# Hybrid trunk layer: one division per pair of attention heads, mixer A's scores in bank pairs, keys stacked by transfers

## The chip, the cores and the metric

The kernel runs on one core of one Trainium2 chip. A core has TensorE (PE, matrix multiplies into PSUM; its weight loads are shown as PEld), VectorE (DVE), ScalarE (ACT), GpSimd (POOL) and SyncE (SP), which here only issues transfers. The metric is the device time of one execution in microseconds (us). Before the change it is 999.15 us, the median of three runs (996.32 to 1001.0).

## What is computed

One layer of a transformer-like trunk for 640 tokens (128 context tokens, 512 latent tokens on a grid of 8 by 64), width 1024. After a modulated RMSNorm one projection gives queries, keys and values of two attention mixers (A: 8 query heads on 2 key heads; B: 8 heads, a 2-D neighbourhood with a learned bias) and two gates. Latent queries also read 128 cached context keys. The outputs of both mixers are merged under the gates, and an MLP follows.

```
def one(qblk):                                     # mixer A, 128 queries at a time
    s = einsum('bqgrd,bkgd->bgrqk', qblk, k) * scale
    p = softmax(s, axis=-1)
    return einsum('bgrqk,bkgd->bqgrd', p, v)
...
p = softmax(concatenate([s_loc, s_ctx], axis=-1))  # mixer B, per grid row
o = einsum('bhqn,bnhd->bqhd', p[..., :n_loc], vr)
return o + einsum('bhqk,bkhd->bqhd', p[..., n_loc:], ctx_v)
...
m = sigmoid(ga) * (a_o @ w_br_a) + sigmoid(gb) * (b_o @ w_br_b)
x = x + g1 * (m @ w_out)
x = x + g2 * _mlp(_rmsnorm(x, n2) * (1 + sc2) + sh2, w1, w2)
```

## The kernel before

Activations lie with features on the 128 partitions and the 640 tokens along the free axis, in two halves of 320 (`HT`, `HALVES`). Matrix products are made from float32r parts: each operand is split into a high and a low part (`wh`, `wl`, `h..h`, `h..l`), and `gemm_k` (L335) makes three matmuls of 320 columns for each of eight blocks of 128 features, so 24 matmuls make one half of a weight tile and 48 a tile. A weight tile is loaded by SP (`wst`), its high part written by ACT (L301), its low part by POOL or DVE (L302). Up to three tiles are held.

In order of the program: a first stage projects the tiles of mixer A's keys, first query pair and values (`FIRST`) while the modulation is computed; the attention stage follows (L504 to L957); then merge, output projection and MLP (from L960).

The attention stage is a list of units: for each pair j of heads `HeadA(2j)`, `HeadA(2j+1)` and the context queries `CtxPair("a", j)`, then the same for B. `attention` (L922) walks in steps. In one step it writes down a T of the unit before, an S of the unit at hand, the value product (`pv`) left by the last step, and then filler.

- S (L630, L686): scores of 128 latent queries against 640 keys (A) or 384 to 512 (B) on PE, the row maximum on DVE, `exp` with the row sum on ACT, and `normalise` (L617), in which DVE takes the reciprocal of the sum and multiplies the whole row block `pa` or `pb` by it. A's scores lie in two single banks, so maximum and `exp` come in two pieces that small DVE operations put together (L643, L646).
- T (L651, L705): PE transposes four blocks of 128x128 into the bank `pt`, ACT and DVE split them into `ph` and `pl`, and `pv` multiplies them by the values into `po`. After a head's last `pv`, `combine` (L611) adds the two halves of `po` into `AO` or `BO`.
- Filler (`fill_tile`, L789) is the projection of tiles that come later: 19 tiles, of which `GATES` are stored to memory for the merge. `STEP` says how much filler a step gets.

PSUM has eight banks in one pool `pp`: two of `g` (projections), three of `s` (scores), two of `t` (transposes), one of `o` (`po`). Keys are needed twice over, on partitions 0 to 63 and 64 to 127, for each of two heads: `k_both` (L569) writes both copies for A by ACT and DVE, in pieces of 64 partitions; `k_part` and `k_dup` write one for B and copy it by a transfer on POOL's queue.

The code is no fixed order in this stage: a scheduler of the framework orders the instructions of every engine by the written order and by when it reckons their inputs ready. Each engine then takes its list in order, and an instruction that waits holds up all that stand behind it on its engine.

## Time and profile before

| what | us |
|---|---|
| median of three runs | 999.15 |
| the profiled execution | 996.88 |
| its span, first to last instruction | 994.9 |
| first stage, until the filler begins | 55.8 |
| start of attention, until the first score | 19.9 |
| units of mixer A | 141.9 |
| units of mixer B, and on to the merge's first product of attention outputs | 145.4 |
| merge, output projection, MLP | 632 |

The stages were cut where PE changes its work: the first filler matmul starts at 55.8 us, the first score (L640) at 75.7, the first score of B (L693) at 217.6, the first matmul that reads a split attention output (`osh`) at 362.9. A profile is read here from the engine with the most work: for each stage, how long PE was idle, what ended each wait, and at what clock it ran. "Granted clock" (PEclk) is 1.00 at full speed.

### The profile page before, as it was taken

How to read it: one execution, taken by the hardware profiler on the slowest of the kernel's cores; microseconds unless marked ns; L12 is line 12 of the kernel's file. 1: busy time of each engine (PE TensorE's matmuls, PEld its weight loads, DVE VectorE, ACT ScalarE, POOL GpSimd, SP SyncE). 2: the span in 40 equal slices, each digit the busy share in tenths (PEclk: the TensorE clock that was granted, in tenths of full speed). 3: DMA queues.
4: the chain of work that ended last, by engine and by line, in shares of the span. 5: the costliest groups of instructions: out<-in, count | busy, mean ns of one | idle time of the engine just before them, and what ended most of it. 6: DMA issues, size and time to landing. Idle time of an engine off the chain costs nothing.

```text
span 994.9 us, 16602 instructions
## 1 busy us (share of the span) xinstructions
PE 950.5 (96%) x6343; PEld 907.5 (91%) x6343; DVE 703.6 (71%) x1577; ACT 517.0 (52%) x1117; POOL 172.0 (17%) x153
## 2 busy tenths in 40 slices
PE   8979899998899999999999999999999999999996
PEld 7767778887788999999999999999999999999996
DVE  4578777788866788788677786778833884368644
ACT  5475667666655654644433564247611663156542
POOL 0351233111222010200041200012200220012100
PEclk9998999999999999999999999999999999999998
DMA  9952110312542455654742253312321233121313
GB/s 345 213 185 58 31 44 25 77 41 80 135 105 76 133 173 172 222 164 155 240 127 86 65 158 110 89 48 85 105 74 35 86 106 88 62 73 34 110 39 107
DMA packets 34768, 108.49 MB, mean 109 GB/s; under 512 B 4320, under 2 KB 8032, under 8 KB 34688
## 3 DMA queue, kind: packets, MB, share of 16 engines
q1 hardware_dynamic: 27072, 82.63, 26.7%
q0 software_dynamic: 6464, 23.47, 8.0%
q8 instruction: 50, 0.82, 0.4%
q10 hardware_dynamic: 1152, 1.31, 0.4%
q14 instruction: 30, 0.25, 0.1%
HBM read 99.14 MB, written 4.60 MB: 104 GB/s over the span
## 4 chain that ended last, share of the span: by engine, by line
PE 68%; DVE 14%; ACT 8%; DMA 5%; issue 4%; POOL 1%; SPq 0%; POOLq 0%; ACTq 0%; DVEq 0%
PE pg L339 7%; PE pg L340 7%; PE pss L341 7%; PE pg L341 7%; PE pss L340 7%; PE pss L339 7%; PE pt L340 4%; PE pt L341 4%; PE pt L339 4%; DMA ms<-wmodA 3%; DVE sr L260 3%; ACT wb L280 2%; PE pt L654 1%; ACT wh L301 1%; DMA wst<-w 1%
## 5 line engine op out<-in xcount | busy, mean ns | idle before, releaser
L301 ACT ACTIVATE wh<-wst 128x1024 fp32r<-128x1024 f32 x84 | 88.8, 1057 | 113.7 <-PE pg L340 41.3
L302 DVE TENSOR_TENSOR wl<-wst,wh 128x1024 fp32r<-128x1024 f32 x53 | 64.8, 1222 | 63.2 <-ACT wh L301 63.1
L302 POOL TENSOR_TENSOR wl<-wst,wh 128x1024 fp32r<-128x1024 f32 x31 | 74.6, 2407 | 158.0 <-ACT wh L301 158.0
L993 DVE SCALAR_TENSOR_TENSOR mt<-wmt,cb 128x512 f32<-128x512 f32 x128 | 81.4, 684 | 0.0
L281 POOL TENSOR_TENSOR wb<-wst,wb 128x512 fp32r<-128x512 f32 x24 | 31.8, 1323 | 260.6 <-ACT wb L280 236.2
L341 PE MATMUL pss<-hidh,wl 128*128 128x320 f32 x216 | 67.0, 310 | 3.4 <-POOL wl L302 3.4
L339 PE MATMUL pss<-hidh,wh 128*128 128x320 f32 x216 | 66.7, 309 | 0.0
L340 PE MATMUL pss<-hidl,wh 128*128 128x320 f32 x216 | 66.7, 309 | 0.0
L608 DVE TENSOR_TENSOR pl<-pt,ph 128x512 fp32r<-128x512 f32 (+2 forms) x80 | 50.2, 632 | 19.5 <-ACT ph L607 18.3
L607 ACT ACTIVATE ph<-pt 128x512 fp32r<-128x512 f32 (+2 forms) x80 | 44.3, 555 | 31.7 <-PE pt L654 15.9
L280 ACT ACTIVATE wb<-sr 128x512 fp32r<-128x512 f32 x48 | 29.8, 626 | 51.5 <-DVE sr L260 37.6
L1162 DVE TENSOR_TENSOR hidl<-rl,hidh 128x320 fp32r<-128x320 f32 x64 | 37.4, 585 | 20.7 <-ACT hidh L1155 20.2
L989 POOL DMA_DIRECT2D wmt<-wmodB x32 | 17.2, 538 | 170.4 <-DVE mt L993 103.3
L281 DVE TENSOR_TENSOR wb<-sr,wb 128x512 fp32r<-128x512 f32 x48 | 36.0, 754 | 14.3 <-ACT wb L280 14.1
L339 PE MATMUL pg<-hidh,wh 128*128 128x320 f32 x144 | 44.5, 309 | 0.0
L340 PE MATMUL pg<-hidl,wh 128*128 128x320 f32 x144 | 44.5, 309 | 0.0
L341 PE MATMUL pg<-hidh,wl 128*128 128x320 f32 x144 | 44.5, 309 | 0.0
L341 PEld LDWEIGHTS pss<-hidh,wl 128*128 128x128 f32 x216 | 40.5, 188 | 4.2 <-POOL wl L302 4.2
L339 PE MATMUL pt<-hidh,wh 128*128 128x320 f32 x136 | 42.0, 309 | 0.0
L340 PE MATMUL pt<-hidl,wh 128*128 128x320 f32 x136 | 42.0, 309 | 0.0
L341 PE MATMUL pt<-hidh,wl 128*128 128x320 f32 x136 | 42.0, 309 | 0.0
L645 ACT ACTIVATE pa<-pss,nm 128x320 f32<-128x320 f32 x64 | 33.2, 524 | 16.3 <-DVE nm L643 16.1
(958 smaller groups left out, 3459.2 us busy)
## 6 DMA issues: line engine op xcount, KB each, us to landing
wst<-w SPq DMA_DIRECT2D x64, 512.0 KB, 3.6
wmt<-wmodB POOLq DMA_DIRECT2D x32, 512.0 KB, 4.1
wst<-w_in SPq DMA_DIRECT2D x31, 512.0 KB, 3.9
ms<-wmodA SPq DMA_DIRECT2D x16, 512.0 KB, 7.5
x<-xT SPq DMA_DIRECT2D x16, 320.0 KB, 6.3
bt<-bias SPq DMA_DIRECT2D x16, 320.0 KB, 3.0
wst<-w_br SPq DMA_DIRECT2D x8, 512.0 KB, 4.2
wst<-w_out SPq DMA_DIRECT2D x8, 512.0 KB, 3.5
```

Source lines behind the costliest of these rows:

```text
L280: ACT.activation(t[:, lo4], src, AF.Copy)
L281: later.append(lambda: (nc.gpsimd if name in BLKP else DVE).tensor_sub(t[:, hi4], src, r32(t[:, lo4])))
L301: ACT.activation(hi, st, AF.Copy)
L302: (nc.gpsimd if key in WPOOLSET else DVE).tensor_sub(lo, st, r32(hi))
L339: PE.matmul(ps, wh[:, k], xh[:, sl], start=first, stop=False)
L340: PE.matmul(ps, wh[:, k], xl[:, sl], start=False, stop=False)
L341: PE.matmul(ps, wl[:, k], xh[:, sl], start=False, stop=last)
L607: ACT.activation(ph[:, :n], pt[:, :n], AF.Copy)
L608: DVE.tensor_sub(pl[:, :n], pt[:, :n], r32(ph[:, :n]))
L645: ACT.activation(p[:, HALVES[j]], ps[j][:, :HT], AF.Exp, bias=nm, accum_out=s2[:, j:j + 1])
L993: DVE.scalar_tensor_tensor(t, st[:, q * 512:(q + 1) * 512], 1.0, r32(cb[2 * q + i][:, :512]), op0=OP.mult, op1=OP.mult, accum_out=parts[:, ...
L1162: DVE.tensor_sub(dst[1][:, sl], r[:, :HT], r32(dst[0][:, sl]))
```

## The change

- **Normalisation.** `normalise` is gone. `exp` writes its row sum into one column of an 8-column tile for the pair (`row_sum`). Once both heads have their sums, `pair_sums` takes one reciprocal and ACT lays it along the free axis as a 128x512 tile `rc`; `pair_norm` transposes `rc` by four PE transposes into a `pt` bank and DVE multiplies the pair's output by it. `rc` comes from the ring of five tiles (`r_`) that `ph`, `pl`, `ct` and `pc` use.
- **Bank pairs.** During mixer A PSUM is divided otherwise: two pairs of banks for scores, two `t`, one `o`, and one `g` instead of two. Maximum and `exp` of a block are one instruction each. With mixer B the old division returns.
- **Keys.** One 128-partition split (`k_split`) makes high and low parts, and six transfers (`k_stack`) lay the copies, on SP's queue for A and on POOL's for B. The cached keys are loaded into the same tile `kr`.
- **Order.** More filler is written ahead of the first score, the gates 21, 29 and 22 move into A's filler list and 30 to the head of B's, `spend` stops at the end of a half during A, squares of the queries are taken ahead of their product, and T is written after the filler. POOL's low parts of these tiles come in two halves. One subtraction for the first query pair moves from POOL to DVE (`Q0P`).

```diff
-AFILL = (1, 10, 2, 6, 3, 14, 21)
-BFILL = (11, 7, 15, 12, 8, 16, 13, 9, 17, 29, 22, 30)
+AFILL = (21, 29, 1, 10, 2, 6, 3, 14, 22)
+BFILL = (30, 11, 7, 15, 12, 8, 16, 13, 9, 17)
-STEP = 2050
-EARLY = 4000
+STEP = {"pa": 2100, "pp": 2500}
+UNIT = 440
-Q0P = 2
+Q0P = 0
...
+    BANKS = {"pp": {"g": 2, "s": 3, "t": 2, "o": 1}, "pa": {"S": 2, "t": 2, "o": 1, "g": 1}}
...
+    def ps_2():
+        return psum["p"].tile([P, 2, 512], F32, tag="S", bufs=2, name="pss")
...
+                    for ks in (slice(0, 4), slice(4, KT)) if key[0] == "in" else (slice(0, KT),):
+                        nc.gpsimd.tensor_sub(lo[:, ks], st[:, ks], r32(hi[:, ks]))
...
+    def k_split(src, n):
+
+        t = kt_tile("kh"), kt_tile("kl")
+        ACT.activation(t[0][:, :n], src[:, :n], AF.Copy)
+        DVE.tensor_sub(t[1][:, :n], src[:, :n], r32(t[0][:, :n]))
+        return t
+
+    def k_stack(t, own, n, q):
+
+        o = kt_tile("kh"), kt_tile("kl")
+        for e in (1 - own, own):
+            for i in range(2):
+                for f in range(2):
+                    if e != own or f != own:
+                        q[i].dma_start(r32((t if e == own else o)[i][half(f), :n]), r32(t[i][half(e), :n]))
+        return (o, t) if own else (t, o)
...
-    def normalise(p, sm):
-        rc = small("rc", 1)
-        DVE.reciprocal(rc, sm)
-        DVE.tensor_scalar(p, p, rc, None, op0=OP.mult)
...
+    def pair_sums(mixer, j):
+        RC[mixer, j] = r_("rc")
+        sm = SUMS[mixer, j]
+        DVE.reciprocal(sm, sm)
+        ACT.activation(RC[mixer, j].rearrange("p (q e d) -> p q e d", q=4, e=2),
+                       sm.rearrange("p (e q) -> p q e", e=2).unsqueeze(3).broadcast_to([P, 4, 2, 64]), AF.Copy)
+
+    def pair_norm(mixer, j):
+
+        rc, o = RC[mixer, j], (AO if mixer == "a" else BO)[j]
+        rows = ps_t()
+        for qt in range(4):
+            PE.transpose(rows[:, qt * P:(qt + 1) * P], rc[:, qt * P:(qt + 1) * P], ident)
+        DVE.tensor_mul(o[:, P:NT], o[:, P:NT], rows)
...
-                DVE.tensor_reduce(n2[:, j:j + 1], ps[j][:, :HT], axis=AX.X, op=OP.max, negate=True)
-            DVE.tensor_tensor(nm, n2[:, 0:1], n2[:, 1:2], op=OP.min)
-            for j in range(2):
-                ACT.activation(p[:, HALVES[j]], ps[j][:, :HT], AF.Exp, bias=nm, accum_out=s2[:, j:j + 1])
-            DVE.tensor_add(sm, s2[:, 0:1], s2[:, 1:2])
-            normalise(p, sm)
+            DVE.tensor_reduce(nm, ps, axis=AX.XY, op=OP.max, negate=True)
+            ACT.activation(p.rearrange("p (a b) -> p a b", a=2), ps, AF.Exp, bias=nm, accum_out=row_sum("a", self.hd, qt))
...
-            ACT.activation(p[:, :w], ps[:, :w], AF.Exp, bias=nm, accum_out=sm)
-            normalise(p[:, :w], sm)
+            ACT.activation(p[:, :w], ps[:, :w], AF.Exp, bias=nm, accum_out=row_sum("b", self.hd, qt))
...
+    ksq = [qk_squares(acc0[0][h], r_) for h in range(2)]
+    F.spend(3 * UNIT)
...
+    AK = k_stack(k_split(kraw, NT + P), 1, NT + P, (DQ[1],) * 2)
...
+    F.spend(6 * UNIT)
     AV, vp = v_stack(vraw, cv[:, 0:P], ps_t)
     for f in vp:
+        F.spend(4 * UNIT)
         f()
-    k_both(AK[1], 1, slice(NT, NT + P), ck[:, 0:P])
-    k_both(AK[1], 1, slice(0, NT), kraw)
-    F.spend(EARLY)
+    F.spend(13 * UNIT)
+    F.half_end()
+    open_banks("pa", "pa")
```

Three places show what this does to the engines' lists. The first is PE at the first scores of mixer A. `pg<-h..,w..` is filler, `pss<-...qs` a score. Before:

```order
L341 MATMUL pg<-h7h,wl 128x320
L640 MATMUL pss<-akh,qs 128x320
L641 MATMUL pss<-akl,qs 128x320
L640 MATMUL pss<-akh,qs 128x320
L641 MATMUL pss<-akl,qs 128x320
L640 MATMUL pss<-akh,qs 128x320
L641 MATMUL pss<-akl,qs 128x320
L535 MATMUL pg<-qsq,pk 128x320
L339 MATMUL pg<-h0h,wh 128x320
```

And now:

```order
L362 MATMUL pg<-h7h,wl 128x320
L687 MATMUL pss<-kh,qs 128x320
L688 MATMUL pss<-kl,qs 128x320
L687 MATMUL pss<-kh,qs 128x320
L688 MATMUL pss<-kl,qs 128x320
L360 MATMUL pg<-h0h,wh 128x320
L361 MATMUL pg<-h0l,wh 128x320
```

Ahead of the first row of scores stood 72 filler matmuls (three halves); now 120 stand there (five halves), and filler comes already after the first block's four score matmuls.

The second place is DVE in mixer A, at the end of the first pair of heads. `n` and `nm` are maxima, `sm` and `s` sums, `pl` the low part of transposed probabilities, `ao` the output. Before:

```order
L642 TENSOR_REDUCE n_1308<-pss 128x1
L608 TENSOR_TENSOR pl<-pt,ph 128x512 x2
L643 TENSOR_TENSOR nm<-n_1308 128x1
L642 TENSOR_REDUCE n_1357<-pss 128x1
L608 TENSOR_TENSOR pl<-pt,ph 128x512
L646 TENSOR_TENSOR sm<-s_1309 128x1
L619 RECIPROCAL rc<-sm 128x1
L620 TENSOR_SCALAR pa<-pa,rc 128x640
L608 TENSOR_TENSOR pl<-pt,ph 128x512
```

And now:

```order
L636 TENSOR_TENSOR pl<-pt,ph 128x512 x4
L689 TENSOR_REDUCE nm<-pss 128x1
L636 TENSOR_TENSOR pl<-pt,ph 128x256
L689 TENSOR_REDUCE nm<-pss 128x1
L643 TENSOR_TENSOR ao_906<-po,ct 64x512
L689 TENSOR_REDUCE nm<-pss 128x1
L643 TENSOR_TENSOR ao_906<-po,ct 64x128
L667 TENSOR_TENSOR ao_906<-ao_906,pt 128x512
```

The five operations that stood between a block's scores and its transposes, beside the maximum, are gone, and one product with the pair's reciprocals (L667) stands behind the pair's outputs.

The third place is PE at the end of the attention stage: the last value products of the context queries (`po<-pl,vst 128x256`) and the gate projections of the merge behind them. Before:

```order
L770 MATMUL po<-pl,vst 128x256
L340 MATMUL pss<-h7l,wh 128x320
L341 MATMUL pss<-h7h,wl 128x320
L339 MATMUL pt<-h0h,wh 128x320
L340 MATMUL pt<-h0l,wh 128x320
L341 MATMUL pt<-h0h,wl 128x320
L769 MATMUL po<-ph,vst 128x256
L770 MATMUL po<-pl,vst 128x256
```

And now:

```order
L666 MATMUL pt<-pk,rc 128x128 x4
L360 MATMUL pss<-h6h,wh 128x320
L361 MATMUL pss<-h6l,wh 128x320
L362 MATMUL pss<-h6h,wl 128x320
L360 MATMUL pss<-h7h,wh 128x320
L361 MATMUL pss<-h7l,wh 128x320
L362 MATMUL pss<-h7h,wl 128x320
L360 MATMUL pt<-h0h,wh 128x320
L819 MATMUL po<-ph,vst 128x256
```

Between the last value product and the first matmul that reads a split attention output stood 69 gate matmuls; now 42 stand there, since more of the gates' work has moved up among the last pair of heads, which have no filler tile left: all 912 filler matmuls stand ahead of the last head's last score, where before 24 were left.

More of the change, by code (lines that the diff above doesn't have):

```diff
@@ L510, in trunk_layer @@
     nc.sync.dma_start(sin, tabs[1])
-    ck, cv = (kp.tile([P, NT], F32, name=x) for x in ("ck", "cv"))
-    nc.sync.dma_start(ck, cacheK)
+    cv = kp.tile([P, NT], F32, name="cv")
     nc.sync.dma_start(cv, cacheV)
@@ L582, in v_cols, with v_stack @@
         return vv[:, :, 0:64], vv[:, :, 64:P]
-    def v_stack(raw, cvp, bank=ps_g):
+    def v_stack(raw, cvp, bank=ps_x):
         v = kp.tile([P, 6 * 256], F32R, tag="V", bufs=2, name="vst")
@@ L853, in __init__ @@
             self.todo = list(AFILL + BFILL)
-            self.allowed = len(AFILL)
+            self.allowed = len([n for n in AFILL if n not in GATES])
             self.cur = None
@@ L884, in spend, with half_end @@
                 self.debt -= c
+        def half_end(self):
+            while self.cur is not None and self.step():
+                pass
         def until(self, what):
@@ L924, in attention @@
         for cur_u in units + [None]:
+            if isinstance(cur_u, HeadB) and "S" in psum["n"]:
+                pend()
+                pend = None
+                F.half_end()
+                while after:
+                    after.pop(0)()
+                open_banks("pp", "pb")
             if cur_u is not None:
@@ L938, in attention @@
                 t, new = 0, None
-                if prev is not None and i < prev.nT:
-                    c, new = prev.T(i)
-                    t += c
+                todo, after[:] = list(after), []
                 if cur_u is not None and i < cur_u.nS:
                     t += cur_u.S(i)
+                tail = prev is not None and i < prev.nT
+                F.spend(max(0, STEP[psum["kind"]] - t - (520 if tail else 0) - (470 if pend else 0) - 500 * len(todo)))
+                if tail:
+                    _, new = prev.T(i)
                 if pend is not None:
-                    t += pend()
+                    pend()
+                for f in todo:
+                    f()
                 pend = new
-                F.spend(max(0, STEP - t))
             prev = cur_u
@@ L950, in attention @@
             pend()
+        while after:
+            after.pop(0)()
     todo = []
```

155 lines of the change are left out of this document (91 added, 64 removed).

## The prediction

> **What bounds the kernel now.** I read the page first, then the busy times of each engine cut at the stages, then who ended PE's waits in the attention stage, then the rows around its longest wait.
>
> ```profile
> span 994.9 us, 16602 instructions
> PE 950.5 (96%) x6343; PEld 907.5 (91%) x6343; DVE 703.6 (71%) x1577; ACT 517.0 (52%) x1117; POOL 172.0 (17%) x153
> ...
> 55.80:75.70 19.90, 13.80 (x87) 12.41 (x86) 15.62 (x25) 14.91 (x35) 9.57 (x8) 0.96 0.60 215
> 75.70:80.70 5.00, 5.00 (x17) 4.61 (x18) 3.13 (x9) 1.87 (x7) 0.00 (x0) 0.50 0.00 0
> 104.80:109.40 4.60, 3.33 (x15) 2.72 (x15) 2.85 (x9) 3.10 (x9) 2.99 (x2) 0.63 0.23 50
> 75.70:217.60 141.90, 129.40 (x776) 112.82 (x777) 114.73 (x301) 94.17 (x255) 34.57 (x24) 0.97 0.17 45
> 217.60:363.00 145.40, 137.48 (x891) 125.94 (x891) 108.26 (x293) 92.35 (x226) 27.39 (x27) 1.00 0.38 106
> 363.00:995.00 632.00, 618.64 (x4193) 615.17 (x4191) 436.69 (x895) 288.37 (x551) 85.41 (x75) 1.00 0.34 108
> ```
>
> The second group's columns: the stretch in us, its length, the busy time of PE, PEld, DVE, ACT and POOL (x instructions), the granted clock, the share of the DMA engines, GB/s. PE bounds the kernel: 96% busy over the span, and after 363 us it is idle for 632.00 - 618.64 = 13.4 us in 632. The change touches nothing there. What it can win lies in three stages: PE is idle for 6.1 us of the start, 141.90 - 129.40 = 12.5 us of mixer A, 145.40 - 137.48 = 7.9 us of mixer B. Twice the granted clock falls: 0.50 for the 5.0 us after the first score, which costs 2.5 us of work at full speed, and 0.63 for 4.6 us at 104.8, which costs 1.7. Together 30.7 us: no version of the attention stage with the same PE work can win more.
>
> ```profile
> PE pss L640 <- DVE qs L561: 6.1, 1, 6.1
> PE pt L654 <- DVE pa L620: 4.8, 9, 1.1
> PE pss L640 <- ACT pa L645: 3.0, 4, 1.4
> PE po L662 <- DVE pl L608: 1.9, 3, 1.0
> PE pt L654 <- DVE pl L608: 1.3, 1, 1.3
> ...
> PE po L769 <- DVE bo L615: 2.6, 2, 1.4
> PE po L662 <- DVE pl L608: 1.6, 1, 1.6
> PE pt L711 <- DVE nm L699: 1.6, 3, 0.9
> PE po L723 <- DVE pl L608: 1.1, 2, 0.9
> ```
>
> Each row is PE's waiter, who ended the wait, the sum in us, how often, the longest. The first five are A with the wait for its first score, the last four B. Nearly all name DVE, which is busy for 114.73 of A's 141.90 us (81%). The row for L620 is the multiplication by the reciprocal itself: the transposes of a block wait for it.
>
> **The start.** Before, the first score stands behind 72 filler matmuls and waits 6.1 us for a query part. DVE and POOL meanwhile:
>
> ```profile
> 67.64 0.82 DVE L574 TENSOR_TENSOR akl<-raw,akh 64x640 fp32r<-64x640 f32 x1
> ...
> 70.01 2.32 DVE L567 TENSOR_TENSOR akl<-ck,akh 64x128 fp32r<-64x128 f32 x1
> ...
> 74.82 0.82 DVE L561 TENSOR_TENSOR qs<-raw,qs 64x640 fp32r<-64x640 f32 x1
> ...
> 69.80 2.38 POOL L302 TENSOR_TENSOR wl<-wst,wh 128x1024 fp32r<-128x1024 f32 x1 [2.86 <-ACT wh L301]
> ...
> 98.31 0.31 PE L339 MATMUL pg<-h2h,wh 128*128 128x320 f32 x1
> ...
> 99.78 0.31 PE L340 MATMUL pg<-h5l,wh 128*128 128x320 f32 x1
> ...
> DMA to landing us min/median/max: 2.7/5.8/7.5
> ```
>
> The last two PE rows are the first and last of eleven filler matmuls in a row: (99.78 - 98.31) / 10 = 0.147 us each. Now 120 of them precede the first score, 48 more than before: 48 x 0.147 = 7.1 us of work, which now lies where PE waited 6.1. Is the new chain ready by then? Before, the first key half was split by 68.46 us; DVE then wrote the other key half's copies ahead of the query parts, which ended at 75.64. Those copies (0.82 us at 67.64, 2.32 at 70.01, two more before 74.82) are gone, 4 to 5 us of DVE, so the query parts end near 71 us. The four transfers for the first head's keys follow the split at some 67 us; copies of this kind from POOL's queue took 2.7 to 7.5 us to land (last row, L578), so they land between 71 and 76, and PE arrives at about 55.8 + 17.6 (filler) + 1.5 (norm products and transposes) + 0.8 (the clock at 0.96) = 75.7. I take no wait: **-6.1, and -2.5** for the clock behind it. If the transfers are as slow as the slowest row and queue, 2 us of wait come back; the ends are -9 and -4.
>
> A 64x128 subtraction took 2.32 us there, beside 0.27 elsewhere, while POOL worked from 69.80 to 72.18. The Trainium skill (GPSIMD Engine Reference, Specifications) says that POOL shares its SBUF interfaces with VectorE, in contention for operations with two SBUF inputs. The row agrees; by it the new key split and the query subtraction that comes to DVE could be held once by a half conversion, some 1.2 us by the row for a whole one, which is inside the range above.
>
> **Mixer A.** The durations (busy us in all, mean ns of one):
>
> ```profile
> L620 DVE TENSOR_SCALAR pa<-pa,rc 128x640 f32<-128x640 f32 x32 | 18.7, 584 | 0.3
> L619 DVE RECIPROCAL rc<-sm 128x1 f32<-128x1 f32 x64 | 10.1, 158 | 9.8 <-ACT pb L700 9.1
> L646 DVE TENSOR_TENSOR sm<-s 128x1 f32<-128x1 f32 x32 | 10.1, 314 | 3.2 <-ACT pa L645 3.1
> L643 DVE TENSOR_TENSOR nm<-n 128x1 f32<-128x1 f32 x32 | 7.0, 219 | 0.2
> L642 DVE TENSOR_REDUCE n<-pss 128x1 f32<-128x320 f32 x64 | 30.8, 484 | 11.0 <-PE pss L641 10.4
> L615 DVE TENSOR_TENSOR ao<-po,ct 64x512 f32<-64x512 f32 x8 | 5.4, 681 | 1.8 <-ACT ct L614 1.7
> L620 DVE TENSOR_SCALAR pb<-pb,rc 128x512 f32<-128x512 f32 x16 | 9.9, 618 | 0.1
> L620 DVE TENSOR_SCALAR pb<-pb,rc 128x384 f32<-128x384 f32 x16 | 8.5, 533 | 0.2
> ```
>
> DVE loses 18.7 of products, 32 x 0.158 = 5.1 of reciprocals, 10.1 and 7.0 of small additions. Sixty-four maxima of 320 columns become 32 of 640, which the trace does not show: one costs between 0.484 and 0.968 us, and I take 0.80, so 5.2 saved. It gains four products like the L615 row, 2.7. That is 43 us off 115, and A's DVE share falls to about 55%. So the 4.8 us of L620 go; the 3.0 us in which a score waits for an `exp` to free its bank are halved, as two blocks fit in the banks where one and a half did; the 3.2 us for `pl`, a product late in DVE's list, are halved too: 4.8 + 1.5 + 1.6 = 7.9 of the 12.5. The stall before 104.8 was one of these, so its clock goes as well: **-7.9 and -1.7** (ends -4.8 and -14.2).
>
> A clock rule is to be weighed here. The row first: the clock fell to 0.63 behind a wait of 1.4 us (the longest of L640 on ACT). The Trainium skill (TensorE: Matmul & The Clock Gate, Part 1: The HAM clock gate) has the clock fall after an idle window of about 3.4 us. By that only the start's 6.1 us would cost clock and the sum would be 1.7 us smaller; I go by the row.
>
> **Mixer B.** DVE loses 9.9 + 8.5 of products and 5.1 of reciprocals and gains 2.7. The waits for `pl` (1.6 + 1.1) are halved, the 1.6 us behind the bias loses the products that stood in its list, say 1.0, and the 2.6 us for `combine` stay, as `po` still has one bank: **-2.3** (ends 0 and -5.3).
>
> **What it adds.**
>
> ```profile
> 94.69 0.60 PE L654 MATMUL pt<-pk,pa 128*128 128x128 f32 x4
> 95.04 0.48 PE L661 MATMUL po<-ph,vst 128*128 128x512 f32 x1
> ...
> L814 ACT ACTIVATE raw<-pg 128x320 f32<-128x320 f32 x30 | 12.9, 433 | 4.3 <-PE pg L341 4.2
> L607 ACT ACTIVATE ph<-pt 128x512 fp32r<-128x512 f32 x56 | 33.3, 597 | 21.3 <-PE pt L654 15.9 <-PE pt L711 4.8 <-PE po L661 0.3
> ...
> 353.29 0.28 DVE L615 TENSOR_TENSOR bo<-po,ct 64x128 f32<-64x128 f32 x1 [0.90 <-ACT ct L614]
> ...
> 359.50 0.82 DVE L350 TENSOR_TENSOR osl<-ao,osh 128x640 fp32r<-128x640 f32 x1
> ...
> 352.67 0.28 PE L770 MATMUL po<-pl,vst 128*128 128x256 f32 x1
> ...
> 362.90 0.31 PE L339 MATMUL pss<-osh,wh 128*128 128x320 f32 x1
> ```
>
> Four transposes take 95.04 - 94.69 = 0.35 us, so the 32 new ones are **+2.8** of PE (none of it hidden, PE being the bound). Their ACT copy, 8 x 0.6, lies in ACT's idle third.
>
> One `g` bank: 15 halves of filler start in A, and each must wait until ACT has copied the half before it out (0.433, plus what stands ahead of it on ACT, such as one `ph` of 0.597). PE's new list has score, transpose or value work between any two of these halves, 0.7 to 2.6 us of it by the prices above, 1.6 on average. So most copies are covered; I take 0.2 us a half, **+3.0** (ends 0 and +13).
>
> The ring of five: `rc` holds one tile while `ph`, `pl` (twice) and `pc` fill the rest, so the next `pl` waits for a `pv`. This touches about four steps of each of eight pairs, most with filler beside it: **+1.0** (0 to 3). The last pair of B has no filler tile: **+1.5** (0 to 4).
>
> The end: the first merge product reads eight splits that DVE makes one after the other behind the last `combine`; the seventh ended at 359.50 + 0.82 = 360.3, 7.6 us after the last value product began (352.67), and PE came to it at 362.9. Now 42 instead of 69 gate matmuls lie between, 6.2 us instead of 10.2. The product needs the seventh split only at its tenth matmul, 1.3 us on, so cover is 6.2 + 1.3 + 0.1 = 7.6: just enough, **0** (to +1.3).
>
> **Sum:** -8.6 - 9.6 - 2.3 + 2.8 + 3.0 + 1.0 + 1.5 = -12.2. The profiled execution took 996.88 us, which gives 984.7; it lies 2.3 below the median of the runs, 999.15, which would give 987. I say **986**.
>
> **Rivals.** *The single bank takes it back (slower).* The place is A's filler: each half waits for its copy-out. The price is 15 times the copy's wait beyond what PE finds to do; if ACT comes to the copy 0.8 us later than PE needs it, this costs 12 us and the rest of the gain is gone; at 1.2 us, with the short cover of 0.7 us between two of the halves and clock losses behind each, 18 to 20: 1004. For it: ACT is 66% busy in A (94.17 of 141.90) and takes its list in order. Against it: PE's list leaves 1.6 us on average, and one combined `exp` replaces two.
>
> *DVE was not the cause.* If PE's waits only move from L620 to `exp` and `ph`, both on ACT, then A keeps its 12.5 us and B its 7.9, the start gains 8.6 and the additions cost 8.3: 997 by the profile's own time, 999 by the median, no change.
>
> *Everything opens.* If nearly all of the 20.4 us of idle time in A and B go and the copies are covered, 996.9 - 30.7 + 2.8 + 3 = 972.
>
> *The transfers are late.* As the key copies at their slowest, with the weight loads on SP's queue in front: the start gives 4 instead of 8.6 and the clock falls again, 991. This is inside my forecast's range.
>
> **How the numbers follow.** The forecast (978 to 993, the late transfers among it) has 0.60, everything opens 0.17, no change 0.15, slower 0.08. The range leaves out the slower case and half of no change: 972 to 999. A measurement of this kernel tells about 0.5% from no change, that is 994.2 to 1004.1. Faster by more: 0.60 + 0.17 = 0.77; within it 0.15 and an eighth of the slower case, 0.16; slower 0.07.
>
> **What would show it.** Right: the first score starts at 75 to 77 us with no wait of over 2 us before it and a clock near 1.00 behind it; PE's idle time in A is 4 to 8 us with L697 no longer waiting for DVE's products; DVE's share of A is near 55%; the first `osh` matmul starts 10 to 14 us earlier than 362.9; after it the two runs are alike. Wrong: waits of filler (L360, first block) on ACT's `raw` copies of several us in sum (the bank), a wait of PE on key transfers at the start, or a long idle stretch ahead of the first `osh`.

## The result, and the profile after

| | median us | lowest to highest | runs |
|---|---|---|---|
| before | 998.72 | 996.32 to 1001.0 | 4 |
| after | 975.64 | 974.41 to 977.37 | 4 |

The ratio is 0.977, with a 95% interval of 0.9743 to 0.9798: the change takes away 23.1 us. The forecast was 986, so the direction and the range (972 to 999) held, and the gain was nearly twice the 12.2 us of the sum. The profiled execution took 975.83 us, close to the median.

The first lines are those of the changed kernel's page, the second fence has its busy times by stage (stretch, length, PE, PEld, DVE, ACT, POOL, granted clock, DMA share, GB/s). The stages are cut as before: first filler, first score of A, first score of B, first matmul on a split attention output, end.

```profile
span 973.7 us, 16415 instructions
PE 944.0 (97%) x6375; PEld 909.6 (93%) x6375; DVE 650.7 (67%) x1335; ACT 503.1 (52%) x1030; POOL 184.5 (19%) x188
```

```profile
56.95:77.26 20.31, 20.31 (x135) 19.66 (x134) 12.35 (x20) 12.25 (x27) 13.34 (x13) 1.00 0.86 272
77.26:82.26 5.00, 5.00 (x37) 5.00 (x36) 1.65 (x2) 2.68 (x6) 0.28 (x1) 1.00 0.56 186
77.26:210.42 133.16, 124.65 (x791) 112.70 (x790) 85.27 (x139) 88.81 (x194) 36.30 (x33) 0.99 0.18 53
210.42:340.08 129.66, 128.58 (x860) 121.29 (x859) 83.08 (x210) 83.18 (x198) 34.57 (x48) 1.00 0.47 129
340.08:973.70 633.62, 619.77 (x4194) 615.19 (x4192) 441.60 (x902) 291.87 (x560) 85.20 (x75) 1.00 0.34 107
```

Length less PE's busy time is its idle time. At the start it went from 6.1 us to nothing (20.31 of 20.31), and the clock behind the first score is 1.00 where it was 0.50. In mixer A it went from 12.5 to 133.16 - 124.65 = 8.5 us, in mixer B from 7.9 to 129.66 - 128.58 = 1.1. The last stage is 633.62 us, 632.00 before.

What ended PE's waits (waiter, releaser, sum in us, times, longest), first in A, behind the "..." in B:

```profile
PE po L704 <- DVE ao L643: 2.0, 1, 2.0
PE pg L360 <- DVE qs L580: 1.9, 1, 1.9
PE pg L360 <- ACT kr L874: 1.2, 1, 1.2
PE pss L687 <- POOL qs L586: 1.0, 1, 1.0
PE pt L697 <- DVE pl L636: 0.6, 2, 0.4
PE pss L687 <- ACT pa L690: 0.5, 1, 0.5
PE po L704 <- ACT ph L635: 0.4, 1, 0.4
PE po L705 <- DVE pl L636: 0.2, 1, 0.2
PE pg L360 <- ACT raw L876: 0.2, 1, 0.2
...
PE po L769 <- DVE nm L746: 0.6, 1, 0.6
PE po L705 <- DVE pl L636: 0.2, 1, 0.2
PE pg L360 <- DVE vst L628: 0.2, 1, 0.2
```

The 4.8 us for the product are gone, and of the 3.0 us for the exponential 0.5 are left. The waits of the first filler matmul of a half (L360) have grown, to 1.9 + 1.2 + 0.2 = 3.3 us in A; before they were 1.3 (L339). New is the wait for `combine` in A, 2.0 us.

**Idle time is not all that PE loses.** The prediction's rows show that records of 0.31 us each start 0.147 us apart: they overlap, so a matmul can start late and no gap is seen. A second count avoids that. Each matmul is given the shortest pitch seen from its start to the next start: 0.147 us for 320 columns, other widths in proportion, 0.35 / 4 = 0.088 for a transposition. The sum of the pitches is the work, and the stretch less the work is what PE lost.

| stage, us | start | A | B | from first filler to first `osh` |
|---|---|---|---|---|
| length before | 19.9 | 141.9 | 145.4 | 307.2 |
| work before | 12.1 | 109.9 | 126.6 | 248.6 |
| lost before (of it idle) | 7.8 (6.1) | 32.0 (12.5) | 18.8 (7.9) | 58.6 (26.5) |
| length after | 20.3 | 133.2 | 129.7 | 283.1 |
| work after | 19.2 | 111.0 | 121.2 | 251.4 |
| lost after (of it idle) | 1.2 (0) | 22.1 (8.5) | 8.5 (1.1) | 31.8 (9.6) |

So the span fell by 21.2 us: 6.6 less lost at the start, 9.9 in A, 10.3 in B, 2.8 more work, 1.2 more until the first filler and 1.6 more in the last stage (58.6 - 31.8 - 2.8 - 1.2 - 1.6 = 21.2). Those last two are not from the change's steps as far as the runs tell: over all kernels below the first filler began at 55.0 to 58.4 us with the same work ahead of it. What the clock costs is part of what is lost: where the granted clock falls in the middle of these profiles, it falls to 0.50 for 3.41 us or a multiple of it, and 3.41 us at 0.50 cost 1.7 us of work.

### The profile page after: what moved, and what is told of

The parts are those of the page before. It is cut to its first block, busy times and chain, and to the rows that moved or that the text cites. A ratio compares the mean times of both kernels' runs of the same rounds, so it can differ in the third digit from the quotient of the medians.

```text
span 973.7 us, 16415 instructions
## 1 busy us (share of the span) xinstructions
PE 944.0 (97%) x6375; PEld 909.6 (93%) x6375; DVE 650.7 (67%) x1335; ACT 503.1 (52%) x1030; POOL 184.5 (19%) x188
## 4 chain that ended last, share of the span: by engine, by line
PE 72%; DVE 10%; ACT 7%; DMA 5%; issue 3%; POOL 1%; SPq 0%; POOLq 0%; DVEq 0%; ACTq 0%
PE pg L360 8%; PE pg L362 8%; PE pg L361 8%; PE pss L362 7%; PE pss L360 7%; PE pss L361 7%; PE pt L362 4%; PE pt L360 4%; PE pt L361 4%; DMA ms<-wmodA 3%; DVE sr L277 3%; ACT wb L297 2%; PE pt L697 1%; ACT wh L318 1%; DMA wst<-w 1%
## 5 line engine op out<-in xcount | busy, mean ns | idle before, releaser
L321 POOL TENSOR_TENSOR wl<-wst,wh 128x512 fp32r<-128x512 f32 (+1 forms) x50 | 79.3, 1600 | 159.7 <-ACT wh L318 159.6
L360 PE MATMUL pss<-hidh,wh 128*128 128x320 f32 x216 | 66.8, 309 | 0.0
L360 PE MATMUL pg<-hidh,wh 128*128 128x320 f32 x144 | 44.5, 309 | 0.0
L360 PE MATMUL pt<-hidh,wh 128*128 128x320 f32 x136 | 42.0, 309 | 0.0
L361 PEld LDWEIGHTS pss<-hidl,wh 128*128 128x128 f32 x216 | 40.5, 188 | 0.0
```

The lines of the kernel that those rows point to most:

```text
L321: nc.gpsimd.tensor_sub(lo[:, ks], st[:, ks], r32(hi[:, ks]))
L360: PE.matmul(ps, wh[:, k], xh[:, sl], start=first, stop=False)
L361: PE.matmul(ps, wh[:, k], xl[:, sl], start=False, stop=False)
```

## The experiments

Twelve kernels ran, four at a time on one chip with the kernel before, which had medians of 997.37, 998.44 and 998.06 us. The changed kernel ran beside the kernel before at 998.72, so differences from its 975.64 below hold to some 1.4 us. "Lost" is counted as above, in the one profiled execution of each kernel.

| kernel | median us | ratio to before (95%) | lost: start | A | B |
|---|---|---|---|---|---|
| before | 998.72 | 1 | 7.8 | 32.0 | 18.8 |
| after | 975.64 | 0.977 (0.9743 to 0.9798) | 1.2 | 22.1 | 8.5 |
| norm_alone | 987.72 | 0.9904 (0.9885 to 0.9923) | 8.2 | 25.5 | 12.8 |
| no_norm | 989.84 | 0.9922 (0.9904 to 0.9939) | 1.1 | 26.6 | 18.4 |
| no_norm_b | 986.78 | 0.9891 (0.9873 to 0.991) | 1.1 | 23.6 | 17.6 |
| load_only | 990.14 | 0.9921 (0.99 to 0.9943) | 1.1 | 26.1 | 17.9 |
| no_pairs | 980.5 | 0.9826 (0.98 to 0.9851) | 1.1 | 27.7 | 8.4 |
| pair_two | 978.8 | 0.9806 (0.9791 to 0.982) | 1.1 | 25.1 | 8.5 |
| old_keys | 980.7 | 0.982 (0.9792 to 0.9847) | 3.0 | 22.8 | 9.9 |
| late_fill | 979.87 | 0.9826 (0.9805 to 0.9846) | 4.3 | 24.2 | 8.8 |
| old_fill | 978.57 | 0.9805 (0.9777 to 0.9833) | 6.3 | 22.6 | 8.0 |
| t_first | 972.47 | 0.9743 (0.972 to 0.9766) | 1.1 | 17.3 | 8.4 |
| t_first_wide | 974.47 | 0.9762 (0.9745 to 0.9778) | 1.2 | 21.9 | 10.0 |
| t_first_dve | 971.92 | 0.9743 (0.972 to 0.9766) | 1.1 | 19.6 | 8.4 |

The theory after the first reading of the traces (D in the expectations): the division on DVE was the main cost in both mixers, in B too, where the forecast had given it little. Its rival (O): the gain came from the order and the keys.

### The division by itself

norm_alone is the kernel before with the division by pairs and nothing else:

```diff
-            DVE.tensor_add(sm, s2[:, 0:1], s2[:, 1:2])
-            normalise(p, sm)
+            DVE.tensor_add(row_sum("a", self.hd, qt), s2[:, 0:1], s2[:, 1:2])
...
+                    if self.e:
+                        after.append(lambda: pair_norm("a", self.j))
...
+            if t == 1 and self.e:
+                pair_sums("a", self.j)
...
-            ACT.activation(p[:, :w], ps[:, :w], AF.Exp, bias=nm, accum_out=sm)
-            normalise(p[:, :w], sm)
+            ACT.activation(p[:, :w], ps[:, :w], AF.Exp, bias=nm, accum_out=row_sum("b", self.hd, qt))
```

> The kernel before with the division per pair of heads alone (two single score banks, keys, filler lists and written order as before). Theory D (the gain in mixers A and B is the work taken off VectorE's list): A and B together gain 20 us against their own TensorE work in the changed kernel, and most of it shows here: 982 to 988 us, the start unchanged (first score still behind a wait of about 6 us). Rival O (it is the written order and the filler lists): no gain beyond noise and the 2.8 us of added transposes, 997 to 1002.

no_norm and no_norm_b are the changed kernel with the old division of each block, in both mixers and in B alone:

```diff
-            ACT.activation(p[:, :w], ps[:, :w], AF.Exp, bias=nm, accum_out=row_sum("b", self.hd, qt))
+            ACT.activation(p[:, :w], ps[:, :w], AF.Exp, bias=nm, accum_out=sm)
+            normalise(p[:, :w], sm)
```

> The changed kernel with each block of probabilities divided by its own sum again, in both mixers. Theory D: 11 to 17 us come back, 987 to 993 us, and TensorE's waits name the product with the reciprocal again. Rival O: at most 4 us, and 2.8 us of transposes are saved: 973 to 979.

> The same in mixer B alone. Theory D: B's gain of 10 us over its own TensorE work is mostly this: 981 to 985 us. Rival O: B gained by its filler lists and order: 974 to 978.

The division alone made the kernel 9.6 us faster than the kernel before on its chip (987.72 against 997.37); taken out of the changed kernel, it cost 14.2. In B alone taking it out cost 11.1, more than either theory had. The busy times by stage, of norm_alone in A and B, then of no_norm_b in B:

```profile
75.25:210.67 135.42, 127.39 (x782) 112.26 (x782) 102.02 (x245) 95.63 (x257) 33.53 (x23) 0.98 0.17 44
210.67:352.85 142.18, 139.31 (x917) 129.37 (x917) 94.04 (x240) 95.55 (x230) 27.86 (x28) 1.00 0.39 113
```

```profile
211.05:348.40 137.35, 131.26 (x844) 121.60 (x843) 92.42 (x263) 79.35 (x190) 34.58 (x48) 0.98 0.43 118
```

With the old division in B PE is idle there for 137.35 - 131.26 = 6.1 us, 1.1 in the changed kernel, and loses 17.6 us, 8.5 there. So in the finished kernel the division is worth more in B than in A (no_norm is only 3.1 above no_norm_b). Of no_norm_b's 11.1 us, 3.8 lie behind the stage: its last stage takes 637.4 us, 633.6 in the changed kernel, with 1.9 us more of waiting for a merge weight and one fall of the clock (1.7). One part of the expectation did not come: PE's waits hardly name the division again (0.4 us for its reciprocal in no_norm, 0.2 us for its product in no_norm_b); in B they mostly name `pl`, `vst` and the maxima, which DVE does as well.

### DVE's time, or the wait of the transposes?

The old division did two things: it filled DVE, and it stood between the exponential and the transposes. load_only puts DVE's work back without the second. Every part of the output is still computed; the added numbers go nowhere.

```diff
+    def unused(p, sm, n):
+        rc, mx = small("rc", 1), small("mx", 1)
+        DVE.reciprocal(rc, sm)
+        DVE.tensor_reduce(mx, p[:, :n], axis=AX.X, op=OP.max)
...
+            unused(p, row_sum("a", self.hd, qt), 416)
...
+            unused(p, row_sum("b", self.hd, qt), 416 if w == 512 else 352)
```

> The changed kernel with DVE's old work put back beside the chain: after each block's exponential DVE takes the reciprocal of the sum and reads 416 or 352 columns of the block into one unused number (as long as the old product by the groups before, 0.53 to 0.62 us), and nothing waits for it. Theory L (what the division cost was DVE's time: its list was too long for PE's pace): most of what no_norm lost comes back, 985-992 us. Theory C (what it cost was that the transposes waited for the product): 974-979 us.

It took 990.14 us, 14.5 above the changed kernel and as much as no_norm, although no transpose waits for the added work. First its busy times in A and B, then three groups of DVE in both (busy, mean ns | idle time ahead, and what ended it):

```profile
76.03:213.11 137.08, 125.51 (x792) 111.18 (x790) 99.94 (x203) 89.80 (x194) 34.97 (x33) 1.00 0.17 50
213.11:352.19 139.08, 133.62 (x860) 124.04 (x859) 96.67 (x272) 81.53 (x195) 34.60 (x48) 0.98 0.44 118
```

```profile
L650 DVE TENSOR_REDUCE mx<-pa 128x1 f32<-128x416 f32 x32 | 18.2, 568 | 0.0
...
L649 DVE RECIPROCAL rc<-sm 128x1 f32<-128x1 f32 x64 | 10.4, 163 | 32.6 <-ACT pa L695 16.9 <-ACT pb L753 14.5
L650 DVE TENSOR_REDUCE mx<-pb 128x1 f32<-128x416 f32 x16 | 9.1, 567 | 0.0
```

In B DVE is busy for 96.67 of 139.08 us, 70%, and PE still loses 9.4 us more than in the changed kernel. The reciprocals show why a share of 70% is enough: DVE stood idle for 32.6 us ahead of them until the exponentials came, with the maxima of the next blocks and the splits `pl` queued behind. Two waits of load_only in B go with it; the second is shown for the changed kernel as well:

```profile
PE pt L764 <- ACT pb L753: 4.3, 5, 1.6
ACT pb L753 <- DVE nm L752: 22.5, 20, 2.3
```

```profile
ACT pb L747 <- DVE nm L746: 11.9, 13, 2.2
```

PE's transposes waited 4.3 us for exponentials, a wait that the changed kernel does not have in B, and ACT waited 22.5 us, 11.9 there, until DVE had the maxima ready. Theory L holds, in the form that an instruction on an in-order engine costs its duration and its wait. How the 14.5 us divide between the two was not tried.

Where the time is lost says more. The changed lists put all filler ahead of the last pair's last scores; the stretch from the last of the 912 filler matmuls to the first `osh` is, in the changed kernel, in no_norm_b and in load_only:

```profile
310.67:340.08 29.41, 29.25 (x194) 26.42 (x193) 23.24 (x57) 22.16 (x52) 3.73 (x7) 1.00 0.32 108
```

```profile
313.56:348.40 34.84, 32.28 (x186) 27.75 (x185) 23.34 (x67) 19.67 (x47) 3.73 (x7) 0.90 0.25 76
```

```profile
314.45:352.19 37.74, 33.36 (x194) 29.21 (x193) 26.05 (x71) 20.77 (x49) 3.75 (x7) 0.91 0.24 75
```

It is 5.4 us longer in no_norm_b, which has eight transposes (0.7 us) less to do there, and 8.3 us longer in load_only, whose matmuls are the same. So of the 9.1 and 9.4 us that B loses more in these two kernels, some 6 and 8 lie in this last stretch, where PE has no filler to cover a late DVE, and 3.4 of them are the clock (6.83 us at 0.50). What the division costs in the finished kernel is thus in large part what it costs without filler; norm_alone, with the old lists, is the better measure of it where filler is left (6.0 us less lost in B).

### The bank pairs

```diff
-            ps = ps_2()[:, :, :HT]
+            ps = [ps_s()[:, :HT], ps_s()[:, :HT]]
...
-            DVE.tensor_reduce(nm, ps, axis=AX.XY, op=OP.max, negate=True)
-            ACT.activation(p.rearrange("p (a b) -> p a b", a=2), ps, AF.Exp, bias=nm, accum_out=row_sum("a", self.hd, qt))
+                DVE.tensor_reduce(n2[:, j:j + 1], ps[j], axis=AX.X, op=OP.max, negate=True)
+            DVE.tensor_tensor(nm, n2[:, 0:1], n2[:, 1:2], op=OP.min)
+            for j in range(2):
+                ACT.activation(p[:, HALVES[j]], ps[j], AF.Exp, bias=nm, accum_out=s2[:, j:j + 1])
+            DVE.tensor_add(row_sum("a", self.hd, qt), s2[:, 0:1], s2[:, 1:2])
...
-    F.half_end()
-    open_banks("pa", "pa")
```

That is no_pairs. Without `half_end` its filler also stops elsewhere: 99 matmuls of it stand ahead of the first score, 120 in the changed kernel. pair_two makes the same six instructions for a block but keeps the pairs of banks (`ps = ps_2()[:, :, :HT]`, pieces `ps[:, j]`), and so the single `g`.

> The changed kernel with mixer A in the old banks: three single score banks, two `g` banks, two maxima, a minimum, two exponentials and a sum for each block; the division by pairs, the keys and the lists stay as changed. Theory P (the bank pairs win by taking instructions off DVE and ACT): DVE's share of mixer A goes from 64% to above 70%, and the time to 979-984 us. Rival G (the second `g` bank gives back about what the pairs bring: in the changed kernel PE waited 3.3 us at mixer A's first projection matmuls, and those waits go): 973-977 us.

> The changed kernel with mixer A's bank pairs kept, but each block in two maxima and two exponentials again, put together by a minimum and a sum. Theory I (the pairs win by fewer instructions on DVE and ACT): as slow as no_pairs or slower, 979-984 us, since the single `g` bank stays too. Theory B (they win by room, two blocks in flight in place of one and a half): 975-978 us.

no_pairs took 980.5 us, 4.9 above the changed kernel; of what PE loses only A's part grew (27.7, 22.1 there). pair_two took 978.8, 3.2 above and just short of theory I's bound; again only A grew (25.1). Mixer A in no_pairs, then in pair_two:

```profile
75.61:215.26 139.65, 129.48 (x797) 115.26 (x796) 97.69 (x234) 96.87 (x258) 37.25 (x32) 0.98 0.19 54
```

```profile
78.28:214.38 136.10, 127.19 (x791) 111.08 (x790) 96.24 (x235) 97.44 (x258) 37.17 (x33) 1.00 0.18 50
```

DVE's share is 70% and 71%, 64% in the changed kernel. Splitting the maximum and the exponential alone costs 3.2 us, with the banks as they are; giving up the pairs as well, and getting the second `g` bank back, costs 1.7 more, which is within what these runs tell apart. In the profiles the clock falls twice in no_pairs' A, for 3.41 us each, and not in pair_two's, which is more than that difference. So fewer instructions look like the main part; that the room of a second pair brings anything is not shown. The rival that the single bank gives back what the pairs bring fell.

### The keys and the filler at the start

old_keys restores `k_both`, `k_part`, `k_dup` and the cached keys' tile; late_fill puts the start's filler behind the chain in one piece; old_fill restores the old lists:

```diff
-    AK = k_stack(k_split(kraw, NT + P), 1, NT + P, (DQ[1],) * 2)
+    AK = [(kt_tile("akh"), kt_tile("akl")) for _ in range(2)]
+    for g in range(2):
+        k_both(AK[g], g, slice(NT, NT + P), ck[:, 0:P])
+        k_both(AK[g], g, slice(0, NT), kraw)
```

```diff
-    F.spend(3 * UNIT)
...
-    F.spend(6 * UNIT)
...
-        F.spend(4 * UNIT)
...
-    F.spend(13 * UNIT)
+    F.spend(4000)
```

```diff
-AFILL = (21, 29, 1, 10, 2, 6, 3, 14, 22)
-BFILL = (30, 11, 7, 15, 12, 8, 16, 13, 9, 17)
+AFILL = (1, 10, 2, 6, 3, 14, 21)
+BFILL = (11, 7, 15, 12, 8, 16, 13, 9, 17, 29, 22, 30)
```

> The changed kernel with the filler that was written ahead of the first score put behind the start again (one call of 4000). Theory F (the start is won by the filler that stands ahead of the first score): the first score waits again for the keys or queries, 4 to 6 us, and the clock falls behind it: 980 to 985 us. Rival K (the start is won by the shorter key chain): the first score comes earlier and waits under 2 us; 974 to 978.

> The changed kernel with the keys split and stacked as before, by DVE and ACT on both halves, in both mixers. Theory K (the key chain is part of the win: late_fill's first score came 5.1 us earlier than the kernel's before with about 2 us less filler ahead of it, so the chain is some 3 us shorter): the wait of the first score returns at 2-5 us, and the four key posts of mixer B cost another 0-2 us: 978-983 us. Rival F (the filler in front covers the old chain too): 974-977 us.

> The changed kernel with the old order of the projections (the value projection 21 last in mixer A, 30 and 29 late in mixer B). Theory N (the order matters little, the division by pairs and the banks do): 974-978 us. Rival L (mixer B's loss fell because the gating projections come early): mixer B loses 3-6 us more from start to start of PE's matmuls, 979-982 us.

The start in late_fill and its wait, then in old_keys, then in old_fill and its wait:

```profile
56.24:70.59 14.35, 12.29 (x73) 10.35 (x72) 10.38 (x20) 10.19 (x24) 8.02 (x10) 1.00 0.84 275
```

```profile
PE pss L687 <- DMA kh<-kh: 1.5, 1, 1.5
```

```profile
58.14:80.26 22.12, 20.54 (x135) 19.63 (x134) 17.18 (x28) 16.02 (x38) 8.94 (x8) 1.00 0.57 205
```

```profile
56.25:82.28 26.03, 23.46 (x139) 21.75 (x138) 16.79 (x27) 16.00 (x35) 13.86 (x14) 0.93 0.67 205
```

```profile
PE pg L560 <- ACT qsq L553: 2.5, 1, 2.5
```

late_fill has 10.0 us of work ahead of its first score (12.1 in the kernel before), which comes 14.35 us after the first filler matmul (19.9 before) and waits for a key transfer: the new chain is shorter, and without the filler its transfers are what PE waits for. It took 979.87, 4.2 above the changed kernel. The early first score and the wait of under 2 us are as rival K had them, the time lies between K's and F's: the keys by themselves are not enough, the filler must cover them. old_keys lost 1.8 us more at the start and 1.4 in B; its median is 5.1 us higher, of which 1.2 lie ahead of the first filler, where nothing differs but what is loaded and scheduled around it. Its time is in theory K's range, but the expected wait at the first score did not come back: PE's one wait in the start is 1.6 us, in which a filler half waits for ACT's `raw` copy of another. So the filler covers the old chain too. old_fill cost 2.9 us, between the two theories, and not where rival L had it: PE loses 5.1 us more at the start (the last stage, at 632.1 us, gave 1.5 back). The old list's first tile is a query pair, and PE waited 2.5 us for its squares on ACT (the clock fell as well, 0.93 over the start); tile 21 has none. B lost no more with the old lists (8.0 against 8.5), so the rival that the order of the projections won B fell.

### The order within a step, and a faster kernel

t_first is the changed kernel with the step's order as it was: T, then S, then the value product, then filler. (The expectation has the filler ahead of the scores; in the kernel that ran it stands last.)

```diff
-                if cur_u is not None and i < cur_u.nS:
-                    t += cur_u.S(i)
                 tail = prev is not None and i < prev.nT
-                F.spend(max(0, STEP[psum["kind"]] - t - (520 if tail else 0) - (470 if pend else 0) - 500 * len(todo)))
                 if tail:
                     _, new = prev.T(i)
+                if cur_u is not None and i < cur_u.nS:
+                    t += cur_u.S(i)
+                spent = STEP[psum["kind"]] - t - (520 if tail else 0) - (470 if pend else 0) - 500 * len(todo)
...
                 pend = new
+                F.spend(max(0, spent))
```

> The changed kernel with the step's order as before: transposes first, then filler, then the next block's scores. Theory N (with the division gone the exponential is in time in either order): 974-978 us. Rival R (scores must be out one filler earlier so that max and exponential lie beside it): PE waits more for the exponentials (pa, pb) and the maxima, 979-986 us.

It took 972.47 us (972.26 to 972.67), below every run of the changed kernel and below both theories; the two did not run side by side, the kernels before beside them lie 0.3 us apart, and the intervals of their ratios overlap. As far as that goes, this part of the change is a loss of some 3 us. Mixer A of t_first:

```profile
77.15:205.68 128.53, 122.07 (x793) 111.48 (x792) 82.15 (x139) 89.05 (x194) 33.96 (x32) 1.00 0.19 55
```

PE is idle for 6.5 us there (8.5 in the changed kernel) and loses 17.3 (22.1). One place can be seen. In the changed kernel DVE's list and PE's have this from 104 us on (start, duration, and in brackets the idle time ahead), and the window behind it:

```profile
104.68 2.24 DVE L595 TENSOR_TENSOR kl<-kr,kh 128x896 fp32r<-128x896 f32 x1
106.84 0.67 DVE L643 TENSOR_TENSOR ao<-po,ct 64x512 f32<-64x512 f32 x1
...
107.57 0.77 PE L704 MATMUL po<-ph,vst 128*128 128x512 f32 x1 [1.96 <-DVE ao L643]
```

```profile
107.50:110.00 2.50, 2.43 (x7) 2.14 (x8) 1.19 (x3) 1.11 (x2) 2.33 (x4) 0.53 0.55 106
```

The split of B's first keys, one instruction of 2.24 us, stands ahead of `combine`, for which the next value product waits since `po` has one bank; then the clock is 0.53 for 2.5 us (second fence); the fall lasts to 111.04 us and costs 1.7 us of work. The split itself was slow: it ran beside two POOL subtractions (L586, 3.89 us from 104.43), and the one of the four splits of this size that ran without POOL took 1.08 us. In t_first PE's only wait for `combine` in A is 1.1 us, and the clock over the same stretch, 107.5 to 110, is 1.00, as over all of A. An estimate from these figures: 0.9 us of wait and 1.7 of clock, 2.6 of the 4.8 us that A gained. That this comes of the one place, rather than of the order as such, is argued and not shown.

t_first_wide gives each step of A more filler (`STEP` 2350 for 2100); t_first_dve sets `QP = 0`, which moves A's query subtractions (L586) from POOL to DVE.

> t_first with 2350 in place of 2100 as the step of mixer A, so that each step gets some more filler. If mixer A's remaining loss (17.3 us in t_first) is want of cover within a step: 969-972 us. If its filler is only moved, or the last pair of B runs short: 972-977 us.

> t_first with the query subtractions of mixer A (L586) on DVE instead of POOL: one took 1.56 us on POOL and 0.82 on DVE in the changed kernel, and PE waited 1.0 us for one. If DVE has room now (64% of mixer A) and POOL's work slows DVE's: 969-972 us. If DVE's list is still what PE waits for: 973-977 us.

More filler in a step did not help: 974.47 us, with 21.9 lost in A, 1.7 of it in a fall of the clock that t_first does not have. The subtractions on DVE made no difference that can be told (971.92, and the same interval as t_first). t_first is the simplest version whose times all lie below those of both kernels.

## Why the prediction was right, and where its sum was off

- **Start, -6.1 and -2.5.** Right. The wait went whole, the first score came at 77.26 us (75 to 77 was expected, and the filler began 1.2 late), and the clock behind it was 1.00. late_fill showed the risk that had been named, a key transfer 1.5 us late, once its cover was taken away. The forecast rested on the shorter chain as much as on the filler; old_keys shows that the filler alone keeps the first score from waiting.
- **Mixer A, -7.9 of idle time, -1.7 of clock, and +3.0 for the single bank.** Idle time is right within a microsecond in sum, partly by luck: it fell by 4.0, where -7.9 + 3.0 gives -4.9. The waits that the forecast named fell by more, 9.7 us (4.8 for L620, 2.5 for the exponential, 2.4 for `pl`), and 3.4 us came for which it had no term (2.0 for `combine`, 1.0 for POOL's query part, 0.4 for `ph`). The 1.7 us of clock were not won: the fall at 104.8 us went, and one of the same size came at 107.63, behind the wait for `combine`. The waits at L360 are 3.3 us, 2.0 more than before, for which 3.0 had been taken, but 1.9 of them end with DVE and not with ACT's copy: `qs` (L580) is the second reader of the bank. The ring of five (+1.0) shows no wait of PE; on DVE `pl` stood 2.1 us until a value product (L704), which may be the ring. The merged maximum takes 0.821 us (0.80 was taken):

```profile
L689 DVE TENSOR_REDUCE nm<-pss 128x1 f32<-128x640 f32 x32 | 26.2, 821 | 15.0 <-PE pss L688 14.7
L667 DVE TENSOR_TENSOR ao<-ao,pt 128x512 f32<-128x512 f32 x4 | 2.7, 678 | 0.1
```

  DVE's share of A, though, is 64% and not 55%: the forecast took the groups' sums off the stage's busy time, but groups count overlapping records twice. Before, A's groups on DVE added up to some 129 us, and its busy time was 114.73.
- **Mixer B, -2.3, with +1.5 for the last pair. This is the step that failed.** PE lost 10.3 us less there. Idle time alone fell by 6.8 (7.9 to 1.1); the other 3.5 lay in late starts that no idle time shows. The prediction went through B's waits one by one by the name of what ended them, halved those for `pl`, and kept the 2.6 us for `combine`, "as `po` still has one bank". What it missed is what DVE's whole list cost: norm_alone, which takes the division off that list and leaves the rest as it was, shows 6.0 of the 10.3 us, against 2.3 forecast for all of B. The row that points to it had been quoted, L619 with 9.8 us of idle time ahead of it, 9.1 of them until B's exponentials came; the forecast used its 158 ns and not the wait, in which all that stands behind the reciprocal on DVE waits too. `combine` is another matter. Its waits in B, in norm_alone and then in no_norm_b:

```profile
PE po L794 <- DVE bo L615: 1.4, 2, 0.7
```

```profile
PE po L774 <- DVE bo L643: 0.2, 1, 0.2
```

  With the division alone 1.4 of the 2.6 us stay, and with the old division in the changed kernel they do not come back. So something else in the change took at least half of that wait away; what, the runs don't show. Of the 10.3 us, old_keys shows 1.4 for the keys, and 2.9 were not told apart. The term for the last pair without filler was about right: behind the last filler matmul PE lost 3.0 us, 0.9 before, by starts; idle time shows none of it from 320 us on.

```profile
320.00:340.08 20.08, 20.08 (x135) 18.60 (x135) 15.25 (x34) 15.34 (x36) 3.73 (x7) 1.00 0.38 131
```

- **The bound of 30.7 us.** Wrong as it was put. It added idle time by PE's busy records to the clock's loss; counted from start to start, 58.6 us were lost in the attention stage, of which the change won 26.8 and t_first, with 26.8 still lost, 31.8, more than the bound. The Trainium skill (Trainium Kernel Development and Optimization, "Reading a trace") calls matmul busy time a bad metric because matmuls are pipelined, and the busy share of weight loads a good one. The trace agrees: in B PE's busy share was 95% before, which seems to leave 5%, while PEld's was 125.94 of 145.40, 87%, and is now 121.29 of 129.66, 94%.
- **Transposes, +2.8, and the end, 0.** Right: PE has 32 more matmuls (6375 for 6343), which at the prediction's pitch are the 2.8 us from 248.6 to 251.4, and it comes to its first `osh` matmul without a wait. The cover is thin just behind it, at a place that had no term: no_norm, no_norm_b and load_only waited 2.2, 2.2 and 1.7 us there for a merge weight's low part on DVE.
- **The rivals.** *The single bank* cost what was forecast and no more: PE's list had work between the halves, as argued. *DVE was not the cause* fell with load_only. *Everything opens* had the nearest time, 972, and was right in that B opened; A did not.

## What to carry to other kernels

Where several waits of the bounding engine end with one in-order engine, don't price them by name: find the instruction in that engine's list which itself waits, and count its duration and its wait for everything queued behind. Count what a pipelined engine loses from start to start, with the shortest pitch seen as the measure, since its busy records cover late starts. A division that runs over a softmax's rows can be moved to the output and done once for several heads, if the engine that did it is the one others wait for. A late engine costs most where the bounding engine has no filler left to do meanwhile, so a measurement made there says little about the rest.

## What the runs showed of the hardware

- DVE's operations with two inputs in SBUF took longer while POOL worked. From the timeline of the changed kernel:

```profile
67.95 3.73 POOL L321 TENSOR_TENSOR wl<-wst,wh 128x512 fp32r<-128x512 f32 x2 [0.74 <-ACT wh L318]
...
68.75 1.78 DVE L572 TENSOR_TENSOR raw<-rt,rot 128x512 f32<-128x512 f32 x1
...
139.00 2.51 POOL L321 TENSOR_TENSOR wl<-wst,wh 128x512 fp32r<-128x512 f32 x2 [14.89 <-ACT wh L318]
...
140.40 1.65 DVE L571 TENSOR_TENSOR rot<-rot,sin 128x512 f32<-128x512 f32 x1
142.09 0.49 DVE L580 SCALAR_TENSOR_TENSOR qs<-pg,qs 64x320 fp32r<-64x320 f32 x1
```

  The product L571 took 1.65 us beside POOL's conversion, which lasted until 141.51, and L572 1.78; the product L667 above, of the same size with one input in PSUM, took 0.678 on average. Over the whole trace of the changed kernel, the 43 such operations of 128x512 f32 on two inputs in SBUF that ran without POOL took 0.67 to 0.69 us, the three that ran wholly beside it 1.36 to 1.78; the 16 with one input in PSUM that ran beside POOL took 0.67 to 0.69. Behind the stretched L571 stands the `qs` for which PE's filler waited 1.9 us.
- After two waits of PE of the same size the clock did two things: behind the 1.96 us from 105.61 it was 0.50, behind the 1.95 us from 140.78 it was 1.00. Within each of the profiles the falls of the clock begin whole multiples of 3.413 us apart and last 3.41, 6.83 or 10.24 us (before: at 74.09 and 104.81, which is nine such steps). Carried on from the fall at 107.63 us of the changed kernel, these steps cut its time like this (the first column behind the length is PE's busy time, the third from the end the clock):

```profile
104.22:107.63 3.41, 1.21 (x9) 0.72 (x7) 3.31 (x4) 1.39 (x3) 3.26 (x3) 1.00 0.78 202
107.63:111.04 3.41, 3.41 (x11) 2.99 (x12) 1.38 (x2) 1.11 (x2) 2.20 (x4) 0.50 0.64 130
138.35:141.76 3.41, 2.19 (x10) 1.14 (x8) 3.35 (x6) 2.91 (x6) 2.51 (x2) 1.00 0.00 0
141.76:145.18 3.42, 2.45 (x16) 2.48 (x17) 2.86 (x5) 1.48 (x2) 0.96 (x1) 1.00 0.47 153
```

  The first wait lies in one step, in which PE was busy for 1.21 of 3.41 us, 35%; the next step ran at 0.50. The second wait is cut in two by the border at 141.76, and its two steps were busy for 64% and 72%. Of all steps at full clock between 40 and 900 us in the fourteen profiles, each one in which PE was busy for under 51% was followed by a step at 0.50, and none in which it was busy for over 62%; between these both happened.

  The Trainium skill (TensorE: Matmul & The Clock Gate, Part 1: The HAM clock gate) has the clock fall after an idle window of about 3.4 us, and the window running freely. The traces agree on the window's length and on its running freely; but a window in which PE was idle for half of the time was enough.
